# Sums of weights made by adding transfers one pair ahead, T2 ahead of T1, and three couples of the up product as two pairs of blocks

## The chip, the core and the metric

The kernel runs on one core of a Trainium2 chip. The engines named here are PE (TensorE, matrix products, with PEld its weight loads), DVE (VectorE), ACT (ScalarE), POOL (GpSimd) and SP (SyncE, which issues most transfers). The metric is the device time of one execution in microseconds (us); lower is better. Three executions of the kernel before took 824.05 to 824.6 us, with a median of 824.46.

## The reference

One layer of an encoder trunk on x of 512 tokens by 1024 features, all in float32. The weights of the large products are what the change touches.

```python
h = _rmsnorm(x, g_pre_mix)
proj = h @ w_in
q, k, v, g, u, sv, a_ret, a_sgu = jnp.split(proj, list(np.cumsum(IN_SPLITS)[:-1]), axis=-1)
y_ret = _retention_branch(q, k, v, g, ret_decay_logit, w_ret_o)
y_sgu = _sgu_branch(u, sv, sgu_ln_g, sgu_ln_b, w_spatial, b_spatial, w_sgu_o)
merged = jax.nn.sigmoid(a_ret) * y_ret + jax.nn.sigmoid(a_sgu) * y_sgu
x = x + _rmsnorm(merged @ w_out, g_post_mix)
h2 = _rmsnorm(x, g_pre_ffn)
x = x + _rmsnorm(_conv_gated_mlp(h2, w_up, conv_w, conv_b, w_down), g_post_ffn)
```

`_conv_gated_mlp` multiplies by `w_up` (1024 by 2 x 2816), runs a convolution of width 3 over the tokens, gates one half with the other and multiplies by `w_down` (2816 by 1024).

## The kernel before, in words

**Products.** Every float32 operand is split into a high and a low part (`split`, lines 84 to 86: ACT copies the high part, DVE subtracts it from the source), and a product is three matmuls: high x high, high x low, low x high.

**Pairs of blocks.** For u, the two gates, part of the up product and the down product, two blocks of outputs are computed together with seven products in place of eight (Winograd's form of Strassen's scheme). On the side of the weights that takes four blocks and four sums: T1 = B11 + B12, T2 = T1 + B22, T3 = B12 + B22, T4 = T2 + B21 (signs are put on the other side). `Pair` (line 676) runs the seven products of 12 matmuls of 256 columns each in three parts: `part1` four, `part2` one, `part3` two. A plain block is `f_block` (line 665): 24 matmuls of 512 columns.

**The stream of weights.** All weights lie in one array `wall` of 146 tiles of 128 x 1024. A list of `units`, written at lines 90 to 117, gives the order in which they are consumed: `("blk", i)` is a whole tile, a form such as `("T1", i)` is one block of a pair, `q` and `t` are the two units of a block of the down product. `w_get` (line 203) hands out the next unit and prepares those that follow, up to about nine slots of the tag `w4` (nine buffers: a form takes one, a `blk`, `q` or `t` two). Preparing means: SP loads into a tile of the tag `raw` (four buffers), the sums are added, and `split` writes the parts into slots.

- `w_form` (line 156): at `B11` SP loads both tiles of the pair, `a` and `b`. At `T1` DVE adds T1 (line 167) and T3 (line 168), and POOL adds T2 (line 169); at `T4` POOL adds T4 (line 171).
- `w_down` (line 177): `q` is a load of four quarters; `t` adds the fourth quarter to the first two in one DVE instruction (line 186) and two more sums of 256 columns (lines 190 and 191).

**Stages.** In order: q and k; v, sv and g with the retention; u as four pairs in a row, each with its `part3` put off until the next pair's `part1` is done; two gates with four rounds each (`gated_pair`: a pair and two plain blocks); the merge; the product with `w_out` (`Down`, line 818), six of whose eight weight tiles are kept ready; the up product; the down product in two halves of nine blocks, each with two whole tiles besides.

The first gate's results `r` are kept in eight SBUF tiles, and in the second gate POOL adds them (line 806).

**The up product.** It has 22 tiles; tiles 4 to 19 come in eight couples (`COUPLES`). In a couple the first tile is a pair of blocks and the second two plain blocks. `tile_done` then runs the convolution and the gate on DVE and ACT, and after tiles 7, 11, 13 and 17 also `down_forms`, which prepares activations for the down product.

**Order.** Each engine runs its own instructions in order; a transfer is issued by an engine's queue when the semaphores before it allow. Instructions are put in order, and tiles are given free buffers, by the compiler's scheduler.

Of the kernel before, what the change touches and what calls it, by code (L numbers as in the profile page):

```python
# [10 lines left out]
F32 = mybir.dt.float32  # L11
# [18 lines left out]
NBLK = 76  # L30
# [8 lines left out]
COUPLES = [(i, i + 1) for i in range(4, 20, 2)]  # L39

# [7 lines left out]
def tile_block(ctx: ExitStack, tc, xT, x, wall, par, cs, wsp, bsp, gpost, gffn, out):  # L48
# [43 lines left out]
    FORMS = ("B11", "B21", "T1", "T2", "T3", "T4", "B22")  # L92
    units = []
    i = 0
    while i < NW:
# [60 lines left out]
    def w_form(form, i):  # L156

        if form == "B11":
            a, b = raw_tile(), raw_tile()
            nc.sync.dma_start(a, wall[i])  # L160
            nc.sync.dma_start(b, wall[i + 1])
            w_raw["B11"], w_raw["B12"] = a[:, :S], a[:, S:]
            w_raw["B22"], w_raw["B21"] = b[:, :S], b[:, S:]
        elif form == "T1":
            t = raw_tile()
            w_raw["T1"], w_raw["T2"], w_raw["T3"], w_raw["T4"] = t[:, :S], t[:, S:], w_raw["B12"], t[:, S:]
            nc.vector.tensor_add(w_raw["T1"], w_raw["B11"], w_raw["B12"])  # L167
            nc.vector.tensor_add(w_raw["T3"], w_raw["B12"], w_raw["B22"])
            nc.gpsimd.tensor_tensor(out=w_raw["T2"], in0=w_raw["T1"], in1=w_raw["B22"], op=ALU.add)  # L169
        elif form == "T4":  # L170
            nc.gpsimd.tensor_tensor(out=w_raw["T4"], in0=w_raw["T2"], in1=w_raw["B21"], op=ALU.add)
        w = slot("wf", 0, 1088)
        lo, hi = w[:, AT_64 : AT_64 + S], w[:, S + AT_192 : 2 * S + AT_192]
        split(hi, lo, w_raw[form])
        return hi, lo

    def w_down(form, i):
# [5 lines left out]
        else:  # L183
            b, raw = w_raw["q"], raw_tile()
            two = "p (n c) -> p n c"
            nc.vector.tensor_tensor(
                out=raw[:, :512].rearrange(two, n=2), in0=b[:, :512].rearrange(two, n=2),
                in1=b[:, None, 768:].to_broadcast([P, 2, 256]), op=ALU.add,
            )
            nc.vector.tensor_add(raw[:, 512:768], raw[:, :256], b[:, 256:512])  # L190
            nc.vector.tensor_add(raw[:, 768:], raw[:, 512:768], b[:, 512:768])
        w = 768 if form == "q" else 1024
# [483 lines left out]
    class Pair:  # L676
# [27 lines left out]
        def part1(self):  # L704
# [616 lines left out]
```

## Time and profile before

| what | us |
|---|---|
| median of three executions | 824.46 |
| the profiled execution, device time | 827.49 |
| its span in the profile | 825.7 |
| PE busy in it | 815.4 |
| DVE busy | 661.4 |
| ACT busy | 440.8 |
| POOL busy | 101.0 |

The profile shows one execution, so terms worked out from it are made against its own time and then carried to the median. In a row of instructions the figures after the bar are the busy time in all, the mean of one in ns, and the idle time of the engine before them with what ended it. A matmul's own duration (277 ns for 256 columns) overlaps the next one; the time from one to the next is read from chains of them. "Landing" is the time from the issue of a transfer to its completion.

### The profile page before, as it was taken

To read this page: it belongs to the slowest core of one execution; us is meant where nothing else is said; L and a number is where in the kernel's file an instruction comes from. 1 tells how busy PE (TensorE), PEld (TensorE's weight loads), DVE (VectorE), ACT (ScalarE), POOL (GpSimd) and SP (SyncE) were. 2 spreads that over 40 slices of the span, in tenths; PEclk is the share of its full clock that TensorE was granted. 3 is DMA by queue.
4 is the path that set the end of the run, shared out by engine and by line. 5 is a ranking of instruction groups with operands and counts; after the bars stand their busy time and mean duration, and the time that the engine had idled before them with its cause. 6 is when DMAs were issued, how large, how long until landed. Compare 5 with 4: busy or idle time off the path is not lost.

```text
span 825.7 us, 13263 instructions
## 1 busy us (share of the span) xinstructions
PE 815.4 (99%) x5152; PEld 735.0 (89%) x5152; DVE 661.4 (80%) x1101; ACT 440.8 (53%) x771; POOL 101.0 (12%) x102
## 2 busy tenths in 40 slices
PE   9999999999999999999999999999999999999996
PEld 7888888888899999999988898899999998999996
DVE  7489897878797777767765568979899899988967
ACT  6636445546665444444445685556566566544531
POOL 0010000102121111132211211210111200000001
PEclk9999999999999999999999999999999999999999
DMA  8733222212223232222349111322322341233244
GB/s 294 246 116 102 77 77 77 77 52 78 90 102 129 103 102 80 101 101 103 108 166 339 48 55 55 103 102 103 102 103 102 102 154 52 77 115 129 96 147 154
DMA packets 29215, 93.24 MB, mean 113 GB/s; under 512 B 3360, under 2 KB 4000, under 8 KB 29152
## 3 DMA queue, kind: packets, MB, share of 16 engines
q1 hardware_dynamic: 26928, 86.85, 30.2%
q0 software_dynamic: 1360, 4.46, 1.6%
q10 hardware_dynamic: 864, 1.09, 0.4%
q8 instruction: 40, 0.66, 0.3%
q14 instruction: 23, 0.19, 0.1%
HBM read 88.19 MB, written 4.19 MB: 112 GB/s over the span
## 4 chain that ended last, share of the span: by engine, by line
PE 91%; DVE 6%; ACT 1%; issue 1%; DMA 0%; POOL 0%; DVEq 0%; SPq 0%; POOLq 0%; ACTq 0%
PE ps L692 23%; PE ps L217 12%; PE ps L218 12%; PE ps L219 12%; PE ps L1058 8%; PE ps L481 5%; PE ps L480 5%; PE ps L482 5%; PE ps L836 2%; PE ps L837 2%; PE ps L838 2%; PE ps L1074 1%; PE ps L761 1%; DVE fl L86 1%; PE ps L279 1%
## 5 line engine op out<-in xcount | busy, mean ns | idle before, releaser
L86 DVE TENSOR_TENSOR wl<-raw,wh 128x1024 fp32r<-128x1024 f32 (+1 forms) x93 | 109.1, 1182 | 48.9 <-PE ps L692 24.2
L79 ACT ACTIVATE wf<-raw 128x512 fp32r<-128x512 f32 x140 | 85.3, 627 | 102.7 <-PE ps L218 34.0
L86 DVE TENSOR_TENSOR wf<-raw,wf 128x512 fp32r<-128x512 f32 x140 | 111.1, 808 | 23.3 <-ACT wf L79 22.4
L692 PE MATMUL ps<-sh,wf 128*128 128x256 f32 x640 | 119.5, 277 | 0.0
L79 ACT ACTIVATE wh<-raw 128x1024 fp32r<-128x1024 f32 (+2 forms) x95 | 93.3, 993 | 37.4 <-DMA raw<-wall 17.0
L692 PEld LDWEIGHTS ps<-sh,wf 128*128 128x128 f32 x640 | 101.1, 188 | 0.8 <-ACT u L79 0.2
L217 PE MATMUL ps<-h2h,wh 128*128 128x512 f32 (+1 forms) x256 | 92.4, 363 | 0.7 <-ACT h2h L906 0.7
L218 PE MATMUL ps<-h2l,wh 128*128 128x512 f32 (+1 forms) x256 | 92.4, 363 | 0.0
L219 PE MATMUL ps<-h2h,wl 128*128 128x512 f32 (+1 forms) x256 | 92.1, 361 | 0.0
L692 PE MATMUL ps<-sl,wf 128*128 128x256 f32 x320 | 88.8, 278 | 0.0
L480 PE MATMUL ps<-wh,xh 128*128 128x512 f32 x192 | 75.0, 391 | 0.0
L481 PE MATMUL ps<-wl,xh 128*128 128x512 f32 x192 | 74.9, 390 | 0.0
L482 PE MATMUL ps<-wh,xl 128*128 128x512 f32 x192 | 74.8, 390 | 0.0
L169 POOL TENSOR_TENSOR raw<-raw,raw 128x512 f32<-128x512 f32 x20 | 36.2, 1809 | 235.2 <-DVE raw L167 207.8
L1058 PE MATMUL ps<-dl,fh 128*128 128x256 f32 x216 | 60.8, 281 | 0.1
L1058 PE MATMUL ps<-dh,fl 128*128 128x256 f32 x216 | 60.7, 281 | 0.0
L1058 PE MATMUL ps<-dh,fh 128*128 128x256 f32 x216 | 60.7, 281 | 0.0
L692 PEld LDWEIGHTS ps<-sl,wf 128*128 128x128 f32 x320 | 60.0, 188 | 0.6
L219 PEld LDWEIGHTS ps<-h2h,wl 128*128 128x128 f32 x256 | 48.0, 188 | 7.7
L217 PEld LDWEIGHTS ps<-h2h,wh 128*128 128x128 f32 x256 | 47.9, 188 | 7.9 <-ACT h2h L906 1.0
L692 PE MATMUL ps<-xh,wf 128*128 128x256 f32 x288 | 54.2, 278 | 0.0
L218 PEld LDWEIGHTS ps<-h2l,wh 128*128 128x128 f32 x256 | 48.0, 188 | 6.6
(314 smaller groups left out, 2048.9 us busy)
## 6 DMA issues: line engine op xcount, KB each, us to landing
raw<-wall SPq DMA_DIRECT2D x145, 512.0 KB, 3.6
x<-x SPq DMA_DIRECT2D x24, 256.0 KB, 5.9
xT<-xT SPq DMA_DIRECT2D x8, 256.0 KB, 5.4
x<-x POOLq DMA_DIRECT2D x8, 256.0 KB, 2.4
xT<-xT POOLq DMA_DIRECT2D x4, 256.0 KB, 3.6
out<-zg SPq DMA_DIRECT2D x4, 256.0 KB, 2.0
out<-zs ACTq DMA_DIRECT2D x3, 256.0 KB, 3.5
cs<-cs SPq DMA_DIRECT2D x2, 256.0 KB, 4.1
```

Of the source, the lines that this page charges most:

```text
L79: nc.scalar.activation(out=o, in_=i, func=AF.Copy)
L86: nc.vector.tensor_sub(lo, src, as32(hi))
L169: nc.gpsimd.tensor_tensor(out=w_raw["T2"], in0=w_raw["T1"], in1=w_raw["B22"], op=ALU.add)
L217: nc.tensor.matmul(o, ah, bh, start=start, stop=False)
L218: nc.tensor.matmul(o, ah, bl, start=False, stop=False)
L219: nc.tensor.matmul(o, al, bh, start=False, stop=stop)
L480: nc.tensor.matmul(acc[t], xh[k][:, c], wh[:, f], start=k == 0, stop=False)
L481: nc.tensor.matmul(acc[t], xh[k][:, c], wl[:, f], start=False, stop=False)
L482: nc.tensor.matmul(acc[t], xl[k][:, c], wh[:, f], start=False, stop=k == KD - 1)
L692: nc.tensor.matmul(o, w_[:, c], a_, start=first and k == n == 0, stop=k == 3 and n == 2, skip_group_check=True,)
L836: nc.tensor.matmul(o, ah, bh, start=k == 0, stop=False)
L1058: nc.tensor.matmul(o, a_[:, c], w_[:, f], start=j == t == i == 0, stop=j == DP - 1 and i == 2 and n not in (M2, M3, M4), skip_group_check= ...
```

## The change

Six things are done together.

1. *Sums by transfers.* T1 and T3 of a pair are no longer added by DVE. SP loads B11 and B12 side by side into a tile of a new tag `sum` (two buffers), and POOL issues a transfer that adds B12 and B22 to it (`accum_op`). This is asked for one pair ahead, at `B21` of the pair before. `b` keeps B22 in its first half; T2 is put in its second half, T4 in T1's place. In the down product the first two sums of `t` come in the same way, one block ahead. The tag `raw` goes from four buffers to three.
2. *Order of the forms.* T2 is prepared and used ahead of T1; POOL's T4 follows T1's split.
3. *Three couples as two pairs.* For the couples that begin at tiles 4, 8 and 14 (`BOTH`) the second tile is a `Pair` too, and `part3` and `tile_done` are put off until the next pair's `part1`.
4. *`r` goes to DRAM* through POOL's queue and is added in the second gate by an adding transfer instead of POOL's addition.
5. *Room.* `NBLK` goes from 76 to 74, two of the four `c` tiles of the down product move to the tag `tmp`, and the broadcast of `gffn` is asked for later.
6. On the host, the blocks of a pair are laid out as B11, B21 and B12, B22.

```diff
-NBLK = 76
+NBLK = 74
+BOTH = (4, 8, 14)
-    FORMS = ("B11", "B21", "T1", "T2", "T3", "T4", "B22")
+    FORMS = ("B11", "B21", "T2", "T1", "T3", "T4", "B22")
...
             for a, b in COUPLES:
                 pair = [(f, UP0 + 2 * a) for f in FORMS]
+                if a in BOTH:
+                    units += pair + [(f, UP0 + 2 * b) for f in FORMS]
+                    continue
...
+    w_pairs = [i for f, i in units if f in ("B11", "q")]
...
-        return sb.tile([P, 1024], F32, tag="raw", bufs=4, name=nm("raw"))
+        return sb.tile([P, 1024], F32, tag="raw", bufs=3, name=nm("raw"))
+
+    def sums(i, first, more):
+        if i not in w_sums:
+            t = w_sums[i] = sb.tile([P, 1024], F32, tag="sum", bufs=2, name=nm("sum"))
+            n = first.shape[1] * first.shape[2]
+            t = t[:, :n].rearrange("p (b c) -> p b c", b=2)
+            nc.sync.dma_start(t, first)
+            nc.gpsimd.dma_start(t, more, accum_op=ALU.add)
+        return w_sums[i]
+
+    def sums_ahead(i):
+        n = w_pairs.index(i) + 1
+        if n < len(w_pairs):
+            (form_sums if w_pairs[n] < DOWN0 else down_sums)(w_pairs[n])
+
+    def form_sums(i):
+        b, w = wall[i : i + 2, :, :S], wall[i + 1].rearrange("p (b c) -> p b c", b=2)
+        return sums(i, b.rearrange("b p c -> p b c"), w)
+
+    def down_sums(i):
+        w = wall[i].rearrange("p (b c) -> p b c", b=4)
+        return sums(i, w[:, 0:2], w[:, 3:4].to_broadcast([P, 2, 256]))
...
         if form == "B11":
-            a, b = raw_tile(), raw_tile()
+            a, b, t = raw_tile(), raw_tile(), form_sums(i)
             nc.sync.dma_start(a, wall[i])
-            nc.sync.dma_start(b, wall[i + 1])
...
-            nc.vector.tensor_add(w_raw["T1"], w_raw["B11"], w_raw["B12"])
-            nc.vector.tensor_add(w_raw["T3"], w_raw["B12"], w_raw["B22"])
+            nc.sync.dma_start(b[:, :S], wall[i + 1, :, S:])
...
+        elif form == "B21":
+            sums_ahead(i)
             nc.gpsimd.tensor_tensor(out=w_raw["T2"], in0=w_raw["T1"], in1=w_raw["B22"], op=ALU.add)
...
         split(hi, lo, w_raw[form])
+        if form == "T1":
+            nc.gpsimd.tensor_tensor(out=w_raw["T4"], in0=w_raw["T2"], in1=w_raw["B21"], op=ALU.add)
...
-            b, raw = w_raw["q"], raw_tile()
-            two = "p (n c) -> p n c"
-            nc.vector.tensor_tensor(
-                out=raw[:, :512].rearrange(two, n=2), in0=b[:, :512].rearrange(two, n=2),
-                in1=b[:, None, 768:].to_broadcast([P, 2, 256]), op=ALU.add,
-            )
+            b, raw = w_raw["q"], down_sums(i)
             nc.vector.tensor_add(raw[:, 512:768], raw[:, :256], b[:, 256:512])
             nc.vector.tensor_add(raw[:, 768:], raw[:, 512:768], b[:, 512:768])
+            sums_ahead(i)
...
-            self.product(2, self.s("S1"), True)
             o = self.product(0, self.s("S2"), False)
             copy(c1[:, T0], o)
+            self.product(2, self.s("S1"), True)
...
-    r = []
+    r = [dp_.tile([P, S], F32, tag=f"r{j}", name=f"r{j}") for j in range(KD)]
...
-            r.append(b)
+            nc.gpsimd.dma_start(r[2 * j + i], b)
...
-            nc.gpsimd.tensor_tensor(out=t, in0=t, in1=r[2 * j + i], op=ALU.add)
+            nc.gpsimd.dma_start(t, r[2 * j + i], accum_op=ALU.add)
...
+    late = []
+
+    def up_pair():
+        p = Pair(None, lambda: tmp("c"), (h2h, h2l, h2forms))
+        p.part1()
+        for j, q in late:
+            q.part3()
+            tile_done(j, q.t)
+        late.clear()
+        return p
...
         if i in couples:
-            p = Pair(None, lambda: tmp("c"), (h2h, h2l, h2forms))
-            p.part1()
+            p = up_pair()
+            if i in BOTH:
+                p.part2()
+                late.append((i, p))
+                p = up_pair()
+                p.part2()
+                late.append((i + 1, p))
+                i += 2
+                continue
...
-    c11, c12, c21, c22 = c4 = [blk(n="c") for _ in range(4)]
+    c11, c12, c21, c22 = c4 = [f(n="c") for f in (blk, blk, tmp, tmp)]
...
-    gpf = bcast(gffn, "gpf")
+    gpf = []
...
         products(m, j, steps if j == DP - 1 else {})
+        if j == 0:
+            gpf.extend(bcast(gffn, "gpf"))
```

More of the change, by code (lines that the diff above doesn't have):

```diff
@@ L792, in gated_pair @@
         return zip(o, p.t)
-    r = []
+    r = [dp_.tile([P, S], F32, tag=f"r{j}", name=f"r{j}") for j in range(KD)]
     for j in range(KD // 2):
-        for o, t in gated_pair(ogh, ogl, late if j == 0 else None):
+        for i, (o, t) in enumerate(gated_pair(ogh, ogl, late if j == 0 else None)):
             b = blk(n="r")
             v.tensor_mul(b, o, t)
-            r.append(b)
+            nc.gpsimd.dma_start(r[2 * j + i], b)
         mix(2 * j)
```

17 lines of the change are left out of this document (7 added, 10 removed).

## The prediction

> **What bounds the kernel now.** I read the page first, then PE's own waits, then the chain of waits, then stretches of the stage that the change shortens.
>
> ```profile
> span 825.7 us, 13263 instructions
> PE 815.4 (99%) x5152; PEld 735.0 (89%) x5152; DVE 661.4 (80%) x1101; ACT 440.8 (53%) x771; POOL 101.0 (12%) x102
> PE 91%; DVE 6%; ACT 1%; issue 1%; DMA 0%; POOL 0%; DVEq 0%; SPq 0%; POOLq 0%; ACTq 0%
> PE ps L264 <- DVE raw L259: 1.0, 1, 1.0
> PE ps L217 <- ACT h2h L906: 0.7, 1, 0.7
> PE ps L279 <- ACT wh L79: 0.4, 1, 0.4
> PE ps L624 <- DVE o L615: 0.3, 1, 0.3
> PE ps L605 <- DVE o L615: 0.3, 1, 0.3
> ```
>
> PE is busy in 815.4 of 825.7 us, and all its waits before the tail sum to 2.7 us. So the kernel goes faster only if PE gets fewer columns, and slower only if something new makes PE wait. DVE at 80% is an average; by stage:
>
> ```profile
> 541.05:561.55 20.50, 20.50 (x135) 18.56 (x134) 15.63 (x25) 11.14 (x20) 2.93 (x2) 1.00 0.29 103
> 561.55:582.05 20.50, 20.50 (x135) 18.56 (x134) 19.85 (x32) 12.71 (x23) 2.94 (x2) 1.00 0.26 92
> ...
> sum 82.00, PE 82.00 PEld 74.25 DVE 72.05 ACT 48.48 POOL 11.75; mean PE 20.50 PEld 18.56 DVE 18.01 ACT 12.12 POOL 2.94
> ...
> 10.00:20.00 10.00, 10.00 (x46) 8.18 (x45) 9.83 (x25) 8.50 (x12) 0.00 (x0) 1.00 0.92 331
> ...
> 217.00:262.00 45.00, 44.98 (x381) 44.78 (x380) 41.32 (x63) 29.25 (x54) 11.05 (x8) 1.00 0.31 106
> ...
> 734.00:806.00 72.00, 71.90 (x610) 71.91 (x611) 55.13 (x88) 31.93 (x48) 0.54 (x1) 1.00 0.36 126
> ```
>
> The columns are stretch, length, busy time of PE, PEld, DVE, ACT, POOL, granted clock, DMA share, GB/s. The first two rows are one couple of the up product each, and the sum is that of four: exactly 20.50 us a couple, PE never idle, at the full clock. DVE is at 15.6 to 19.9 us of it, the larger figure where `down_forms` falls into the couple. So PE sets the pace, with DVE close behind.
>
> **The couples: the term that pays.** In a couple one tile is a pair of blocks (7 products of 12 matmuls, 256 columns) and the other is two plain blocks (2 x 24 matmuls, 512 columns). For the couples that begin at tiles 4, 8 and 14 the change makes the second tile a pair too.
>
> ```profile
> 541.05 5.45 PE ps L692 x48
> ...
> 551.97 1.37 PE ps L692 x12
> ...
> 556.08 2.73 PE ps L692 x24
> ```
>
> Four products take 5.45, one 1.37, two 2.73: a pair costs 5.45 + 1.37 + 2.73 = 9.55 us. The couple is 20.50 us, so its two plain blocks cost 10.95 (0.228 us a matmul against 0.114: half the columns, half the time). A second pair in their place saves 10.95 - 9.55 = 1.40 us, and three couples save **4.2 us**.
>
> What must hide for that is the second pair's work on DVE.
>
> ```profile
> L86 DVE TENSOR_TENSOR wf<-raw,wf 128x512 fp32r<-128x512 f32 x140 | 111.1, 808 | 23.3 <-ACT wf L79 22.4
> L86 DVE TENSOR_TENSOR wl<-raw,wh 128x1024 fp32r<-128x1024 f32 x81 | 101.6, 1256 | 47.2 <-PE ps L692 24.2 <-issue 9.3 <-PE ps L218 4.8
> L167 DVE TENSOR_TENSOR raw<-raw 128x512 f32<-128x512 f32 x20 | 13.8, 688 | 1.5 <-DMA raw<-wall 1.4
> L168 DVE TENSOR_TENSOR raw<-raw,raw 128x512 f32<-128x512 f32 x20 | 17.1, 853 | 1.0 <-DMA raw<-wall 0.7
> L709 DVE TENSOR_TENSOR c<-ps,c 128x256 f32<-128x256 f32 x8 | 3.3, 417 | 0.0
> ```
>
> Seven splits at 0.808 replace two at 1.256, and three evacuations of 256 columns at 0.417 come in (L709, and its like at L720 and L732): 5.66 - 2.51 + 1.25 = +4.4 us. Against that, every pair loses its two DVE additions for T1 and T3, 0.688 + 0.853 = -1.54. Over the four couples above (two of them to be doubled, six pairs afterwards, four pairs' additions gone) DVE goes from 72.05 busy us to 72.05 + 2 x 4.4 - 4 x 1.54 = 74.7, while PE goes from 82.0 to 79.2. That is 94%: hidden, with 4.5 us to spare in four couples. Without that cover the gain shrinks by what DVE lacks (third rival). T2 before T1 in `part1` puts S2's product one product behind the copy of `b[0]` instead of two; 1.37 us covers an ACT copy of 256 columns. Deferring `part3` is what the u stage already does, and its row above (217 to 262) shows PE at 44.98 of 45. Both cost nothing.
>
> **T1 and T3 by transfers: what is queued behind what.** A pair now asks SP for 512 KB of first halves, and POOL for an adding transfer of 512 KB that waits for them; `b` shrinks to 256 KB. So a pair moves 1.75 MB instead of 1 MB: two in 19.1 us are 192 GB/s (512 KB and its like counted in 1024s), where the stretch from 10 to 20 us carries 331. No adding transfer is in this trace; the nearest rows are
>
> ```profile
> raw<-wall SPq DMA_DIRECT2D x145, 512.0 KB, 3.6
> ...
> xT<-xT SPq DMA_DIRECT2D x8, 256.0 KB, 5.4
> ...
> xT<-xT POOLq DMA_DIRECT2D x4, 256.0 KB, 3.6
> L884 POOL DMA_DIRECT2D x<-x x8: 542/568/589, 451.0 to 482.5; - x8
> L169 POOL TENSOR_TENSOR raw<-raw,raw 128x512 f32<-128x512 f32 x20 | 36.2, 1809 | 235.2 <-DVE raw L167 207.8
> L171 POOL TENSOR_TENSOR raw<-raw,raw 128x512 f32<-128x512 f32 x20 | 26.7, 1333 | 75.2 <-DVE wf L86 71.4 <-ACT cv L955 3.9
> L806 POOL TENSOR_TENSOR sig<-sig,r 128x512 f32<-128x512 f32 x8 | 11.6, 1465 | 36.4 <-DVE sig L805 36.4
> ```
>
> On POOL, T2(i) stands behind the adding transfer of pair i+1, which waits for a first half on SP, which waits for the sum tile that pair i-1 leaves at its T4 split. That round is 3.6 (load) + 0.57 (issue) + 1.81 (T2) + 2 x 0.81 (T2's and T1's splits) + 1.33 (T4) + 2 x 0.81 (T4's copy on ACT, put at DVE's time, and its split) = 10.6 us, against 9.55 us of PE a pair where pairs follow pairs. Such a run is at most four pairs (the u stage), so it loses 3 x 1.05 = 3.2 us out of a lead of seven products (nine slots, two held by the deferred pair), 7 x 1.365 = 9.6 us, of which the unit's own copy and split take some 2. Cost 0; 3.2 us with that lead gone.
>
> The `r` tiles go to DRAM and come back as an adding transfer: 3.6 or more for POOL's 1.465 (L806). Only the last two matter, for mh[6] and mh[7]. `Down` first runs 48 matmuls over k = 0 and 1, 48 x 0.228 = 10.9 us, so this is hidden; uncovered, with a landing of 3.6 to 7.2, it would cost 2 to 6 us once.
>
> **The start.** Three `raw` tiles instead of four, one of them `hold`.
>
> ```profile
> 3.05 0.43 SPq L133 DMA_DIRECT2D raw<-wall  x1
> ...
> 7.86 0.33 SPq L133 DMA_DIRECT2D raw<-wall  x1
> 8.23 0.43 SPq L241 DMA_DIRECT2D xT<-xT  x1
> ...
> 5.23 1.17 PE L279 MATMUL ps<-xh,wh 128*128 128x512 f32 x4 [0.44 <-ACT wh L79]
> ```
>
> The load at 3.05 now waits until 7.86, when block 0's tile is free, and xT[2] behind it on SP. With 3.6 to 4 us to land and a copy and a split of at most 1.26 each it is ready near 14.4. PE needs it after two blocks of 24 x 0.228, at 5.23 + 10.9 = 16.2. Cost 0; bounds -0.3 (the blocks ahead land sooner) and +0.5 (a landing as slow as xT's 5.4, with xT's own split behind the block's).
>
> **The down product: the tight place.** The first two sums of each `t` unit come by transfer (L186, 0.69 us of DVE, 18 times, off PE's path: PE is busy throughout). In return the ring of two sum tiles closes on itself: the `t` split of block j-1 frees the tile; SP loads 256 KB; POOL's transfer adds 256 KB; then DVE's two additions, ACT's and DVE's split of block j+1.
>
> ```profile
> L1141 SPq DMA_DIRECT2D x<-x x8: 320/372/452, 795.6 to 816.4; - x8
> ...
> DMA to landing us min/median/max: 2.8/4.5/5.4
> ...
> 741.47 0.43 DVE L190 TENSOR_TENSOR raw<-raw,raw 128x256 f32<-128x256 f32 x1
> ...
> 743.57 1.23 DVE L86 TENSOR_TENSOR dl<-raw,dh 128x1024 fp32r<-128x1024 f32 x1 [1.21 <-ACT dh L79]
> ...
> 752.71 0.85 ACT L79 ACTIVATE dh<-raw 128x768 fp32r<-128x768 f32 x1 [1.76 <-PE ps L1058]
> ...
> 757.65 0.85 ACT L79 ACTIVATE dh<-raw 128x768 fp32r<-128x768 f32 x1 [1.76 <-PE ps L1058]
> ```
>
> A lone 256 KB load lands in 2.8. The add lands in 3.6 (POOL's plain load, issue included) plus an unknown d. From the first addition to the end of the split are 744.80 - 741.47 = 3.3. Together 9.7 + d us per two blocks; PE takes 2 x (757.65 - 752.71) = 9.88. So the ring fits as long as d is under 0.2 and otherwise falls behind by d - 0.2 every two blocks, 4.5 times in each half of nine blocks. The lead it can eat is three units of 2.47 less a copy and a split of 1.23 each, 5.0 us (nine slots are four units in flight, and a unit's second half waits for the oldest of them); in the first half the two whole blocks add 2 x 48 x 0.114 = 10.9. Bounds for d: 0 (no dearer than a plain load) and 3.6 (a second transfer in full). I take **0.8**, what a second 256 KB costs within one load (3.6 for 512 KB against 2.8), because an add reads as much again: behind by 4.5 x 0.6 = 2.7 us, within the lead, cost 0. At d = 3.6 it is 4.5 x 3.4 - 5.0 = +10.3.
>
> The Trainium skill bears on d. In "Collectives: The Full Stack", section "The bandwidth ceiling: the fold count and why AG ≠ RS ≠ AR", the reduce in a transfer is limited not by the addition but by having two sources to read. By that rule an add costs what a load of twice its size costs, and the sum stays at 820.2, where the upper bound, two transfers in full, would give 830.5; no run here shows it yet.
>
> **The sum.** The profiled execution took 827.49 us: its span of 825.7 and 1.8 around it. It is 3.0 above the median of 824.46. Couples -4.2, all else 0: 821.5 of span, 823.3 for such an execution, and by the median 824.46 - 4.2 = **820.2 us**. Removing the additions could also shorten the two 0.3 us waits on L615; the range's low end takes them, not the sum.
>
> **The rivals.** *The ring of sum tiles in the down product sets the pace (slower).* For it: 9.7 against 9.88 leaves no room, and DVE, being in order, holds other splits behind an addition that waits. Against it: it needs d above 2.3 to eat the gain (4.5 x 2.1 - 5.0 = 4.4) and above 2.6 to end slower by 0.2%. At d = 3.1, 4.5 x 2.9 - 5.0 = 8.0 us: 820.2 + 8.0 = **828**. *POOL's order gives part back in the runs of pairs.* For it: T2 stands behind a wait for two engines. Against it: a lead of 7.6 us. If first halves land at xT's 5.4 and an issue for two rows a partition takes 1.14, the round is 13.0, a pair loses 3.4, three rounds 10.3: 2.7 us are given back, **823**, and up to 824 if the `r` transfers add to it. *DVE binds the doubled couples, and the change doesn't do what it says.* A split beside a POOL addition takes up to 1.78 us instead of 0.69:
>
> ```profile
> L86 DVE TENSOR_TENSOR wf<-raw,wf x140: 674/686/1782, 191.9 to 668.1; 128x512 fp32r<-128x512 f32 x140
> ```
>
> The mean of 0.808 charges that about once a pair; four times a doubled couple at the full 1.1 us adds 3 x 1.1 = 3.3 us to each, so the 4.5 us to spare in four couples with two doubled ones are overdrawn by 2.1, half of the gain or more: **822.3 to 824.5**. The Trainium skill ("SBUF — State Buffer", section "Who interferes with whom") has a DVE instruction with two SBUF inputs fully blocked by a GpSimd one that reads SBUF; the row's 1782 agrees, and T2 and T4 stay on POOL in the new pairs.
>
> **How the numbers follow.** As worked out 60% (818.8 to 822.3); POOL's order 11%; DVE 7%; the ring 18%; something at the start or in the smaller pool of blocks 4%, slower. A change under 0.2%, 1.6 us, can't be told from none. Faster (below 822.8): the first case and a few per cent of the next two, 0.64. Same: most of the second and third, 0.13. Slower: the ring and the last case, 0.23. The range, 818.8 to 828.2, holds the first three cases and the ring up to d = 3.1.
>
> **What would show it.** Doubled couples of 19.1 us with PE never idle, 1.4 shorter each. DVE below 95% there. The adding transfers of 256 KB landing within 4.9 us in the down product (3.6 and a d of up to 1.3), and no PE wait on a DVE split of `dl` there; PE still 99% busy. Wrong would be: PE waits of over 1 us on `wf` or `dl` splits, DVE waits for a DMA into `sum` that repeat from block to block, or the first 20 us growing longer.

## The result, and the profile after

The changed kernel takes 864.58 us (median of four executions, 863.55 to 871.38) against 824.25 us: over all executions a ratio of 1.0508, with a 95% interval of 1.0453 to 1.0562. It is 5% slower, where the prediction had 820.2 us and a range that ended at 828.2.

Lines of the page of the changed kernel, the last four of them transfers with their size and the median us to landing:

```profile
span 861.9 us, 13751 instructions
PE 825.2 (96%) x5260; PEld 746.6 (87%) x5260; DVE 637.1 (74%) x1067; ACT 446.6 (52%) x798; POOL 153.5 (18%) x157
...
sum<-wall SPq DMA_DIRECT2D x23, 512.0 KB, 4.2
sum<-wall POOLq DMA_DIRECT2D x23, 512.0 KB, 5.7
...
sum<-wall SPq DMA_DIRECT2D x18, 256.0 KB, 3.4
sum<-wall POOLq DMA_DIRECT2D x18, 256.0 KB, 4.8
```

And the largest of its waits on PE and one on DVE (in all, times, longest, in us):

```profile
PE ps L716 <- ACT c L80: 11.3, 6, 4.1
PE ps L1100 <- DVE dl L87: 8.2, 5, 3.2
PE ps L716 <- ACT sig L80: 3.4, 1, 3.4
PE ps L1100 <- ACT dh L80: 2.6, 2, 2.1
...
DVE sum L213 <- DMA sum<-wall: 26.0, 9, 6.2
```

PE waited 2.7 us before the tail in the kernel before; here four groups alone make 25.5 us, and they name three places. `c L80` is ACT's copy out of PSUM in the up product, `sig L80` the same copy in the second gate, `dl` and `dh` the splits of the down product. DVE has become less busy (637.1 against 661.4 us): no engine has become the bound; the engines wait for each other.

The time by stages, for the two kernels and the experiments below. A stage runs from the start of its first matmul to that of the next stage's, read from the PE records of each profile; in brackets is the idle time between matmuls (pauses over 0.15 us).

| kernel | u | second gate | couples | down product | span |
|---|---|---|---|---|---|
| before | 45.7 | 76.6 | 161.8 (0) | 112.2 (0) | 825.7 |
| after | 44.2 | 81.9 (3.4) | 175.8 (11.3) | 128.9 (11.5) | 861.9 |
| E1 T1 first | 44.1 | 76.6 | 166.6 (4.9) | 127.9 (11.5) | 848.6 |
| E2 four raw tiles | 52.7 (5.2) | 76.8 | 180.8 (17.3) | 132.6 (13.2) | 876.2 |
| E3 down sums on DVE | 45.0 | 81.4 (3.0) | 175.7 (10.9) | 113.7 (1.3) | 845.7 |
| E4 no doubled couples | 45.5 | 81.2 (2.7) | 161.8 (0) | 131.0 (11.9) | 852.1 |
| E5 T1 first, down sums on DVE | 45.9 | 76.6 | 166.9 (4.5) | 110.5 (1.0) | 829.7 |
| E6 before, doubled couples | 44.6 | 76.6 | 180.2 (12.7) | 109.3 (0.4) | 840.8 |
| E7 before, T2 first | 45.9 | 76.6 | 167.3 (4.5) | 109.0 (0) | 829.5 |
| E8 E1 with three sum tiles | 43.9 | 76.8 | 168.1 (6.8) | 123.6 (8.8) | 843.1 |
| E9 E5, doubled at 4, 10, 16 | 44.7 (0.4) | 78.8 (1.8) | 161.8 (0.8) | 109.1 (0) | 824.4 |
| E10 E5, T2 first in three pairs | 43.9 | 76.6 | 166.7 (5.2) | 110.3 (1.1) | 827.0 |
| E11 E9, T2 first in three pairs | 45.7 | 76.6 | 163.6 (2.7) | 109.1 (0) | 824.7 |
| E12 E8, asked for two blocks ahead | 44.1 | 76.6 | 168.0 (6.7) | 124.9 (10.1) | 846.4 |
| E13 before, T2 first in one u pair | 43.8 | 76.6 | 161.6 (0) | 109.0 (0) | 821.1 |
| E14 E9, T2 first in one u pair | 43.5 | 76.6 | 162.4 (1.6) | 109.1 (0) | 821.4 |
| E15 E1 without the down add | 45.7 | 76.6 | 167.3 (5.9) | 111.8 (0) | 831.3 |

From before to after the span grows by 36.2 us: couples +14.0, down product +16.7, second gate +5.3, u -1.5, all other stages together +1.7. In each of the three stages that grow, the idle time is less than the loss. Most of the rest is the clock: behind these pauses the granted clock falls to half for a while. Two stretches of the same length, behind the pause of 3.53 us at 588 us and a little later (columns as in the prediction's tables of stretches):

```profile
591.70:596.50 4.80, 4.80 (x23) 4.80 (x24) 4.31 (x7) 2.66 (x5) 0.00 (x0) 0.50 0.67 228
597.00:601.80 4.80, 4.80 (x35) 4.43 (x34) 3.87 (x5) 2.95 (x5) 1.20 (x2) 1.00 0.73 241
```

PE counts as busy in both. The first holds 23 matmuls of 256 columns, one every 0.21 us where the full clock gives one every 0.114; the second holds 25 of 256 columns and 10 of 512. The records of the granted clock have six such windows before the tail, five of 3.4 us and one of 6.8. They hold 102 matmuls of 256 columns, each 0.1 us longer than at the full clock: some 10 us that no term of the prediction held. In the second gate and the down product pauses and clock make up nearly all of the loss (3.4 + 1.6 of 5.3 us, 11.5 + 4.5 of 16.7). In the couples they are 11.3 + 4.1 us, against 4.1 us of columns saved; the 2.7 us that are left are a slower pace of PE (last section) and the shortest waits.

**Where PE waits in the couples.** The timeline of the changed kernel around 588 us, first PE, then ACT, then DVE (start, length, instruction, and in brackets the idle time before it with its releaser):

```profile
591.53 0.58 PE L716 MATMUL ps<-sh,wf 128*128 128x256 f32 x1 [3.53 <-ACT c L80]
...
586.92 1.68 ACT L979 ACTIVATE cv<-c,part 128x512 f32<-128x512 f32 x2
588.51 0.36 ACT L80 ACTIVATE c<-ps 128x256 f32<-128x256 f32 x1
588.77 1.04 ACT L80 ACTIVATE wh<-raw 128x1024 fp32r<-128x1024 f32 x1
590.57 0.63 ACT L993 ACTIVATE cv<-cv 128x512 f32<-128x512 f32 x1 [0.76 <-DVE cv L986]
591.11 0.37 ACT L80 ACTIVATE c<-ps 128x256 f32<-128x256 f32 x1
...
587.77 1.93 DVE L982 SCALAR_TENSOR_TENSOR cv<-c,part,cv 128x511 f32<-128x511 f32 x1
589.73 0.75 DVE L986 SCALAR_TENSOR_TENSOR cv<-c,part,cv 128x511 f32<-128x511 f32 x1
```

The product with B21 ended near 588. S2's product comes next and goes into `b[0]`, so it needs the copy of B11's product, which could have run from 586.6 on. But that copy (at 591.11) stands at its place in ACT's order: behind two convolution steps (L979), the copy of an earlier product, a split, and a GELU (L993). The GELU waits for a convolution step on DVE (L986), itself late because L982 took 1.93 us instead of the 0.74 it takes at 590.40; POOL's addition of T4 (L202) ran beside it from 587.56 to 589.13. So what the prediction's third rival speaks of, DVE slowed beside POOL, is one link of this chain, though DVE's work as a whole does not set the pace. The copy takes 0.37 us and is some 4 us late.

### The profile page after: what moved, and what is told of

Its sections match the earlier page's. It is cut to its first block, busy times and chain, and to the rows that moved or that the text cites. A ratio compares the mean times of both kernels' runs of the same rounds, so it can differ in the third digit from the quotient of the medians.

```text
span 861.9 us, 13751 instructions
## 1 busy us (share of the span) xinstructions
PE 825.2 (96%) x5260; PEld 746.6 (87%) x5260; DVE 637.1 (74%) x1067; ACT 446.6 (52%) x798; POOL 153.5 (18%) x157
## 5 line engine op out<-in xcount | busy, mean ns | idle before, releaser
L716 PE MATMUL ps<-sh,wf 128*128 128x256 f32 x736 | 142.1, 284 | 11.3 <-ACT c L80 11.3
L716 PEld LDWEIGHTS ps<-sh,wf 128*128 128x128 f32 x736 | 119.8, 194 | 13.7 <-ACT c L80 12.4
L80 ACT ACTIVATE wh<-raw 128x1024 fp32r<-128x1024 f32 (+2 forms) x89 | 87.0, 987 | 32.9 <-DMA raw<-wall 19.9
L137 POOL DMA_DIRECT2D sum<-wall x41 | 42.4, 1034 | 273.9 <-DMA sum<-wall 152.6
L87 DVE TENSOR_TENSOR wf<-raw,wf 128x512 fp32r<-128x512 f32 x92 | 66.2, 733 | 25.5 <-ACT wf L80 25.3
L80 ACT ACTIVATE wf<-raw 128x512 fp32r<-128x512 f32 x92 | 56.2, 624 | 47.7 <-PE ps L242 23.8
L241 PE MATMUL ps<-h2h,wh 128*128 128x512 f32 (+1 forms) x208 | 73.5, 357 | 0.7 <-ACT h2h L930 0.7
L242 PE MATMUL ps<-h2l,wh 128*128 128x512 f32 (+1 forms) x208 | 73.7, 356 | 0.1
L80 ACT ACTIVATE wf<-sum 128x512 fp32r<-128x512 f32 x69 | 43.0, 627 | 57.8 <-PE ps L716 34.5
L87 DVE TENSOR_TENSOR wf<-sum,wf 128x512 fp32r<-128x512 f32 x69 | 52.7, 770 | 14.2 <-ACT wf L80 13.9
L197 POOL TENSOR_TENSOR raw<-sum,raw 128x512 f32<-128x512 f32 x23 | 41.9, 1822 | 58.0 <-DMA raw<-wall 31.5
```

Of the source, the lines that this page charges most:

```text
L80: nc.scalar.activation(out=o, in_=i, func=AF.Copy)
L87: nc.vector.tensor_sub(lo, src, as32(hi))
L137: nc.gpsimd.dma_start(t, more, accum_op=ALU.add)
L241: nc.tensor.matmul(o, ah, bh, start=start, stop=False)
L242: nc.tensor.matmul(o, ah, bl, start=False, stop=False)
L716: nc.tensor.matmul(o, w_[:, c], a_, start=first and k == n == 0, stop=k == 3 and n == 2, skip_group_check=True,)
```

## The experiments

Every experiment is the changed kernel or the kernel before with the edits shown; ratios are to the kernel before, timed on the same chip.

### E1, E3, E4, E2: one part at a time

E1 puts T1 ahead of T2 again.

```diff
-    FORMS = ("B11", "B21", "T2", "T1", "T3", "T4", "B22")
+    FORMS = ("B11", "B21", "T1", "T2", "T3", "T4", "B22")
...
+            self.product(2, self.s("S1"), True)
             o = self.product(0, self.s("S2"), False)
             copy(c1[:, T0], o)
-            self.product(2, self.s("S1"), True)
```

> The changed kernel with T1 ahead of T2 again, in the list of forms and in the products of part1; all else as changed. Theory Q (order): PE loses time in the couples because the product of S2 now comes one product (1.37 us) after the one whose copy by ACT it needs, and that copy stands in ACT's queue behind a gelu or a split that waits; then PE's waits on ACT's copies of c (11.3 us in the changed kernel) fall below 3, the couples fall from 175.8 to about 160 us and the whole to about 848. Theory R (ring of raw tiles): the weights themselves come late, because three raw tiles make the load of b wait for POOL's T4; then the waits move to the splits and the time stays within 4 us of 864.

Measured 850.59 us, 1.0306 (1.0276 to 1.0336). The second gate is back at 76.6 and the couples fall by 9.2 us, PE's waits for ACT's copy from 11.3 to 3.7 us. The order cost 14.5 us in these two stages. The couples still stand 4.8 us above before and 6.6 above the 160 that theory Q expected, so the order is not the whole cause there.

E3 adds the first two sums of the down product on DVE again, into the same two tiles.

```diff
-    w_pairs = [i for f, i in units if f in ("B11", "q")]
+    w_pairs = [i for f, i in units if f == "B11"]
...
-            b, raw = w_raw["q"], down_sums(i)
+            b, raw = w_raw["q"], sb.tile([P, 1024], F32, tag="sum", bufs=2, name=nm("sum"))
+            two = "p (n c) -> p n c"
+            nc.vector.tensor_tensor(
+                out=raw[:, :512].rearrange(two, n=2), in0=b[:, :512].rearrange(two, n=2),
+                in1=b[:, None, 768:].to_broadcast([P, 2, 256]), op=ALU.add,
+            )
...
-            sums_ahead(i)
```

> The changed kernel, but in the down product the first two sums are added by DVE again, into the same two sum tiles, with no transfer. Theory S (the ring of sum tiles there closes too slowly): the stage from the first down product to the last falls from 128.8 to about 112 us, the whole to about 847. Rival (more traffic or the three raw tiles hold the loads back): it stays above 122.

Measured 845.52 us, 1.0244 (1.0184 to 1.0305). The down product falls from 128.9 to 113.7 us, and the other stages stay within 1 us of the changed kernel.

E4 has `BOTH = ()`.

> The changed kernel with no couple doubled (BOTH empty). If the loss in the couples comes with the doubled ones (deferred tile_done, more splits, theory D), the couples take 162 to 165 us instead of 175.8 and the whole about 853. If it comes from the sums by transfer or the order wherever they are, it stays above 170.

Measured 856.68 us, 1.0379 (1.0296 to 1.0463). Without doubled couples the stage is 161.8 us, exactly that of before, although T2 still stands ahead of T1. So in the changed kernel the order hurts the couples where pair follows pair.

E2 gives `raw` its four buffers back; for room `NBLK` is 72.

> The changed kernel with four raw tiles instead of three (and NBLK 72 to make room). Theory R: the couples fall by 10 us or more, and the 3.4 us gap at the last gate round (ACT waits there for a transfer into raw) goes with its slow clock: about 847. Theory Q: the couples stay at 173 to 176, only the gap at the gate goes, 5 us: about 859.

Measured 876.98 us, 1.0625 (1.0589 to 1.0661): slower than either theory gave, so the three raw tiles are not the cause of the couples' loss. The second gate is back at 76.8 us, though T2 still stands first: there the fourth raw tile does help. With it the losses move to ACT's queue in other places, u among them (52.7 us), and one of them shows the mechanism at its plainest. PE's largest waits in E2, and ACT at 544 us:

```profile
PE ps L716 <- ACT c L80: 17.3, 6, 5.9
...
PE ps L716 <- ACT u L80: 5.2, 1, 5.2
```

```profile
544.38 0.63 ACT L80 ACTIVATE wf<-sum 128x512 fp32r<-128x512 f32 x1 [7.63 <-POOL sum L202]
544.91 0.36 ACT L80 ACTIVATE c<-ps 128x256 f32<-128x256 f32 x1
```

ACT stood idle for 7.63 us, since the instruction at the head of its queue, the split of T4, waited for POOL's addition; the copy that PE needed was next in line. POOL in turn had stood 5.17 us waiting for an adding transfer into `sum`, ahead of T2 and T4; the pause of 5.2 us in u (`u L80`) has the same chain, with 4.83 us of waiting on POOL. Of this E2 shows the chain, not why it is worse here than with three raw tiles.

### E5 to E7: do the parts add up, and what does each do to the kernel before?

E5 is E1 and E3 together.

> The changed kernel with T1 back ahead of T2 and the first two sums of the down product back on DVE; transfers for the other pairs' sums and for r, and the three doubled couples, stay. If the two losses (order Q, ring of sum tiles S) are separate, the stages are those of the two runs before: second gate 76.6, couples 166.6, down product 113.7, in all 848.6 - (127.9 - 113.7) = 834 us of span, 836 us of time. If the ring's lateness in the down product came out of the couples (a rival), taking the order back would have cured part of it twice and the sum of the stages is higher, 840 or more. Neither theory makes it faster than the kernel before (824.3).

Measured 831.18 us, 1.0067 (1.0036 to 1.0099). E1 saved 14.0 us and E3 19.1, and 864.58 - 33.1 is 831.5: as far as the spread of these runs shows, the two losses are separate and add up. The span is 829.7 for the expected 834: the first tiles of the up product (ahead of the couples), 2.9 us longer in E1 than before, are back at their length, the down product is 3.2 us shorter than in E3 (PE's pace, last section), and u 1.8 longer.

E6 is the kernel before with the doubled couples alone: `BOTH`, `up_pair` and `late` as in the change, T1 ahead of T2, all sums by DVE and POOL.

> The kernel before with the three doubled couples alone (T1 ahead of T2, all sums by DVE and POOL, part3 put off as in the change). The term of the prediction, PE alone: couples 161.8 - 4.2 = 157.6, time 820. Theory D (DVE): with T1 and T3 still on DVE, each doubled couple adds 4.4 us for the second pair and 1.54 for its additions, so four couples with two doubled ask 72.05 + 2 x 5.94 = 83.9 us of DVE against 79.2 of PE: DVE then sets the pace there, couples 163 to 165, time 826 to 828.

Measured 843.05 us, 1.0214 (1.0185 to 1.0244), a bigger loss than either theory gave. PE's waits in E6:

```profile
PE ps L696 <- ACT c L80: 10.5, 10, 2.0
PE ps L696 <- DVE wf L87: 2.2, 4, 0.6
```

The couples take 180.2 us. With the sums by transfers (E5) they take 166.9. E5 differs by the transfers and what came with them (three raw tiles, `r` by DRAM, less room). So the transfers do help the up product, by 13 us in this setting; they make room for an edit that does not pay. And the waits are again mostly for the copy, with T1 first: the order is not the only way to expose it.

E7 is the kernel before with T2 ahead of T1 alone.

> The kernel before with T2 ahead of T1 alone (list of forms and part1), no transfers of sums, no doubled couples. Prediction's term: 0, time 824.3. Theory Q (the copy of b[0] is only one product ahead and stands in ACT's queue): exposed where something stands ahead of it on ACT, so the second gate gets its gap of 3 us and its stretch at half clock, +5, while the couples, whose pairs do not follow pairs, stay at 161.8: 829. If instead the gap of the second gate needs the transfers or three raw tiles too, it stays at 824 to 825.

Measured 832.87 us, 1.0097 (1.0064 to 1.0130). The second gate stays at 76.6, so its loss in the changed kernel needs something else of the change as well; E2, where it is gone, points to the three raw tiles. The couples grow by 5.5 us, of which four waits for ACT's copy make 4.5 (2.3 the longest). So on the kernel before, with T1 and T3 on DVE, the order hurts even where a plain block follows each pair; with the sums by transfers it does not (E4).

### E9 to E11: why the doubled couples still lose with T1 first

The change puts doubled couples at tiles 4, 8 and 14; `down_forms` runs after tiles 7, 11, 13 and 17, and falls into the couples at 8 and 14. In E5 PE and ACT at 574 us:

```profile
574.29 0.39 PE L720 MATMUL ps<-sh,wf 128*128 128x256 f32 x1 [1.30 <-ACT c L80]
...
570.98 0.63 ACT L80 ACTIVATE wf<-sum 128x512 fp32r<-128x512 f32 x1 [3.24 <-POOL sum L202]
571.52 0.62 ACT L80 ACTIVATE fh<-gp 128x512 fp32r<-128x512 f32 x1
572.04 0.36 ACT L80 ACTIVATE c<-ps 128x256 f32<-128x256 f32 x1
572.30 0.62 ACT L80 ACTIVATE wf<-raw 128x512 fp32r<-128x512 f32 x1
572.83 0.62 ACT L80 ACTIVATE fh<-fs 128x512 fp32r<-128x512 f32 x1
573.34 0.62 ACT L80 ACTIVATE wf<-raw 128x512 fp32r<-128x512 f32 x1
573.86 0.37 ACT L80 ACTIVATE c<-ps 128x256 f32<-128x256 f32 x1
```

PE waits for the copy at 573.86; ahead of it stand a split that waited 3.24 us for POOL, and `down_forms`' splits (`fh`) among those of the weights. By the order of PE's records the product that waits is S2's of the second pair: S3 of the first pair starts at 567.49, B11 and B21 of the second fill 569.02 to 571.40 (four matmuls of B11 stand ahead of S3), S1 starts at 571.40 and S2 at 574.29. It needs the copy of its own pair's B11, done by 570.1, with two products between. S3 of the first pair, right behind S2 and into the same `b[0]`, waits 0.3 us only. Theory G below takes the waiting product for S3's, which the records do not bear out.

E9 is E5 with `BOTH = (4, 10, 16)` (the first part of the diff below), E10 is E5 with T2 ahead of T1 in the first pair of each doubled couple alone (the other parts), E11 is both.

```diff
-BOTH = (4, 8, 14)
+BOTH = (4, 10, 16)
...
-                    units += pair + [(f, UP0 + 2 * b) for f in FORMS]
+                    units += [(f, UP0 + 2 * a) for f in FORMS2] + [(f, UP0 + 2 * b) for f in FORMS]
...
-            p = up_pair()
+            p = up_pair(i in BOTH)
             if i in BOTH:
```

> The kernel of the run with T1 first and the down product's sums on DVE, with the doubled couples at tiles 4, 10 and 16 in place of 4, 8 and 14. There the couples at 8 and 14 are the ones into which down_forms falls (after tiles 7 and 13); the new places have none. Theory F (the burst of down_forms on DVE and ACT makes the copies late): the waits of 4.5 us in the couples mostly go and the couples fall from 166.9 to 160 or less, time 825. Theory G (a doubled pair has S3 right behind S2, both into b[0], with the copy of b[0] between them, wherever it stands): the couples stay at 165 or more, time 830.

> The kernel of the run with T1 first and the down product's sums on DVE; only the first pair of each doubled couple takes T2 ahead of T1, so that the product with S1 stands between S2 and S3. Doubled couples stay at 4, 8 and 14. Theory G: the two waits of 1.3 and 1.4 us before the S3 products go, couples 166.9 - 2.7 = 164, time 828. Theory F, and the reading of the order in the changed kernel (a copy one product ahead is late wherever ACT has a queue): the waits only move from S3 to S2, couples 166 to 168.

> Both edits of the two runs before together. PE's columns alone give 157.6 for the couples (161.8 - 4.2). If F and G each hold a part of the 9.3 us over that, the couples come to 158 to 161 and the time to 821 to 824.5, at or just under the kernel before (825.3 on the chip of the last runs). If the pace of PE or DVE is what is left, 163 or more.

E9 measured 826.02 us, 1.0024 (1.0003 to 1.0046), its couples 161.8; E10 830.63, 1.0090 (1.0067 to 1.0112), couples 166.7; E11 826.35, 1.0025 (1.0007 to 1.0042), couples 163.6. The place is worth 5 us, as theory F has it, although the 160 us or less that F expected were not reached. The order inside the first pair is worth nothing. E10's edit leaves the product that waits in E5, S2 of the second pair, as it was: it still waits 0.6 and 1.0 us, and S2 of the first pair now waits as well (0.35 and 0.93). So theory G was not tested at the place that costs. Both together (E11) are no better than the place alone, and the 158 to 161 us hoped for did not come.

In E9 the stage has the 4.1 us of columns less and is as long as before all the same. Going from the start of one matmul to the next, intervals that are over 0.15 us too long make 1.7 us of the difference, and 3.0 us are spread over all the others: a slower pace of PE in its runs of pairs, of which the last section tells.

### E8, E12, E15: the down product

One round of a sum tile in the changed kernel, SP, POOL, DVE and ACT, from the load of its first half to the next load:

```profile
799.17 0.33 SPq L136 DMA_DIRECT2D sum<-wall  x1
803.37 1.22 POOL L137 DMA_DIRECT2D sum<-wall  x1 [3.69 <-DMA sum<-wall]
808.36 0.42 DVE L213 TENSOR_TENSOR sum<-sum,raw 128x256 f32<-128x256 f32 x1
809.41 1.06 ACT L80 ACTIVATE dh<-sum 128x1024 fp32r<-128x1024 f32 x1 [2.36 <-DVE sum L214]
810.50 1.23 DVE L87 TENSOR_TENSOR dl<-sum,dh 128x1024 fp32r<-128x1024 f32 x1 [1.26 <-ACT dh L80]
811.75 0.33 SPq L136 DMA_DIRECT2D sum<-wall  x1
```

First half 4.2, add 5.0, additions and splits 3.4: 12.6 us for a tile that serves every second block, and PE needs two blocks in 9.9. This is one of the shorter rounds: from load to load of the same tile they take 11.3 to 19.3 us in this stage, waits for their turn included.

E8 is E1 with three sum tiles (`NBLK` 72), E12 the same with the sums of the down product asked for two blocks ahead.

```diff
-            t = w_sums[i] = sb.tile([P, 1024], F32, tag="sum", bufs=2, name=nm("sum"))
+            t = w_sums[i] = sb.tile([P, 1024], F32, tag="sum", bufs=3, name=nm("sum"))
...
-        n = w_pairs.index(i) + 1
-        if n < len(w_pairs):
-            (form_sums if w_pairs[n] < DOWN0 else down_sums)(w_pairs[n])
+        n = w_pairs.index(i)
+        for j in w_pairs[n + 1 : n + 2 + (i >= DOWN0)]:
+            (form_sums if j < DOWN0 else down_sums)(j)
```

> The changed kernel with T1 ahead of T2 and three sum tiles instead of two (for that NBLK is 72). Theory S, the round of a sum tile: one round was measured as 12.6 us (first half 4.2 with POOL's wake-up, add 5.0, additions and splits 3.4); for two blocks PE takes 9.9, for three 14.8. With three tiles the ring no longer limits: down product 112 to 114 us instead of 127.9. If the loss lies in the order of waits on DVE, ACT or POOL and not in the number of tiles, it stays above 122. The stages before it may be longer by the smaller pool of blocks; only the down product is read here.

> The kernel with T1 first and three sum tiles, with the sums of the down product asked for two blocks ahead instead of one. With three tiles alone the down product fell only from 127.9 to 123.6, because a request stood behind the block before it in the order of SP. If the lead of the request is what lacks (first half 4.2, add 5.0, additions and splits 3.4 = 12.6 us against 9.9 us for two blocks and 14.8 for three), the down product comes to 112 to 114. If the transfers themselves are too slow, or POOL's and SP's queues hold them up in any order, it stays above 120.

E8 measured 846.36 us, 1.0255 (1.0210 to 1.0300), its down product 123.6 us where 112 to 114 were expected; E12 851.09, 1.0315 (1.0221 to 1.0410), down product 124.9. So neither a third tile nor an earlier request cures it, against the round's own sum. What DVE does in E12:

```profile
790.35 0.43 DVE L213 TENSOR_TENSOR sum<-sum,raw 128x256 f32<-128x256 f32 x1 [4.91 <-DMA sum<-wall]
790.69 0.95 DVE L87 TENSOR_TENSOR dl<-raw,dh 128x768 fp32r<-128x768 f32 x1
791.56 0.42 DVE L214 TENSOR_TENSOR sum<-sum,raw 128x256 f32<-128x256 f32 x1
...
793.64 1.22 DVE L87 TENSOR_TENSOR dl<-sum,dh 128x1024 fp32r<-128x1024 f32 x1
```

The addition of the next block (L213, at 790.35) stands ahead of the splits of the block that PE wants. It waits 4.91 us for its transfer, and the splits, which free the tiles of SP's next loads, stand behind it. DVE waits at L213 in the same way in the changed kernel (26.0 us in all) and in E8 (28.4). That the compiler's scheduler put it so early in E12 because the tile is free earlier is likely, but not shown.

E15 is E1 with the adding transfer left out in the down product.

```diff
-            nc.gpsimd.dma_start(t, more, accum_op=ALU.add)
+            if i < DOWN0:
+                nc.gpsimd.dma_start(t, more, accum_op=ALU.add)
```

> The changed kernel with T1 first; in the down product the adding transfer is left out, so that its first two sums lack the fourth quarter. The first halves still come by SP into two sum tiles. One round of a sum tile with the add measured 12.6 us against 9.9 of PE for two blocks; without it 4.2 (or the landing of 3.5 alone) + 3.4 = 7 to 8 us, so by theory S the down product falls from 127.9 to 109 to 113. If SP's order (a first half behind a load of raw that waits for its tile) is what holds, it stays above 120.

Measured 833.05 us in one execution, down product 111.8 us with no pause. SP's part and its order stayed, and DVE's waits at its additions fell to 2.0 us at most. So the adding transfer, with its issue on POOL, is what makes this stage long; how much of that goes by the length of the round and how much by DVE's queue is open, since three tiles should have cured the first.

### E13, E14: the pace of PE, and the best of both

E13 is the kernel before with T2 ahead of T1 in the first pair of u alone; E14 is E9 with the same edit.

```diff
-            units += pair
+            units += [(f, i) for f in FORMS2] if i == U0 else pair
...
-            p.part1()
+            p.part1(j == 0)
```

> The kernel before with T2 ahead of T1 in the first pair of the u stage alone. Theory P (pace): in a run of 256-column products without plain blocks, one short wait of PE (in the kernel before 0.30 us at 222.4, for ACT's copy of b[0], S3 right behind S2) leaves PE at 118 ns a matmul instead of 113.6 until a plain block or a longer pause comes. With S1 between S2 and S3 the wait does not arise: the stage of 336 matmuls goes from 45.7 to about 44.2 us, as it did in the changed kernel, and the time by -1.5 to 822 to 823.5, the first version under the kernel before. If the pace in the u stage depends on something else (DVE's sums beside it, the transfers), u stays at 45.7 and the time unchanged.

> The changed kernel with T1 first, the down product's sums on DVE, the doubled couples at 4, 10 and 16 (826.0 against 823.8), and T2 ahead of T1 in the first pair of u alone. By theory P u falls from 44.7 to 43.8 to 44.2; with the second gate at 76.6 (it had a wait of 1.8 us) the span is 821.5 to 823.5 and the time within 1.5 us of the kernel before. If the order of ACT's queue changes elsewhere, 825 to 828 as before.

E13 measured 823.51 us, 0.9997 (0.9984 to 1.0009); E14 824.84, 1.0005 (0.9987 to 1.0023). In E13's profile u takes 43.8 us, as theory P has it, but the time does not differ from the kernel before beyond its interval. No version was found that beats it; E14, with the columns saved and all that was found put right, equals it; its couples take 162.4 us, so the saving is not seen there either.

## Why the prediction was wrong, step by step

Three terms that the prediction put at nothing failed: the cover of the doubled couples, the order T2 before T1, and the ring of sum tiles. The stages of the first two grew by 14.0 us (couples) and 5.3 (second gate), that of the third by 16.7 (down product).

- **The columns of the doubled couples, -4.2: right as a count.** In the profiles the couples have 672 matmuls of 256 columns and 372 of 512 before, 924 and 228 after (the last 12 of the stage's last plain block are not in it). At the pace the prediction used (0.114 and 0.228 us) that is 161.4 against 157.3: 4.1 us less.
- **"Hidden, with 4.5 us to spare in four couples": the first failed step.** It weighed DVE's sum of work against PE's. What ran out was not work but order: ACT's copies of 0.37 us stood behind instructions that waited for DVE or POOL. E4 against the changed kernel prices the edit there at +14.0 us; against the couples before, it is +4.8 with T1 first (E1), and 0 away from `down_forms` (E9). Two terms were missing for the gain to come: the burst of `down_forms`, 5 us, and PE's pace, 3.0 us in E9. The u row quoted in the prediction, 381 matmuls in 45.00 us, is 118 ns each; the couple's products, 48 in 5.45, are 113.5. A second pair makes the couple a run of pairs like u, and the sum priced it by the other row.
- **"T2 before T1 ... Both cost nothing": the second failed step.** "1.37 us covers an ACT copy of 256 columns" is true of the copy and not of its place in the queue. Going back gains 9.2 us in the couples and 5.3 in the second gate (E1); alone, the order costs 5.5 us of the couples (E7). In the second gate the copy stood behind three splits of `w_out` that waited for a load:

```profile
416.73 0.63 ACT L80 ACTIVATE mh<-sig 128x512 fp32r<-128x512 f32 x1 [4.33 <-DMA sig<-r]
...
423.22 2.09 ACT L80 ACTIVATE wh<-raw 128x512 fp32r<-128x512 f32 x3 [3.61 <-DMA raw<-wall]
425.22 0.36 ACT L80 ACTIVATE sig<-ps 128x256 f32<-128x256 f32 x1
```

- **The ring of sum tiles, "within the lead, cost 0": the third failed step, and the rival with the right place, given 18%.** The term that was mis-sized is the round, 9.7 + 0.8 = 10.5 us in the prediction and 12.6 in the trace. The first half was put at 2.8, a lone load; with the other loads it takes 3.4 in the median and 4.2 until POOL's add goes out. The add's landing of 4.4 (4.8 measured, d = 1.2) was not far off. With 12.6 the prediction's own formula gives 4.5 x (12.6 - 9.9) - 5.0 = 7 us; PE's pauses were 11.5, and half clock added some 4.5. So the formula has the place right but not the whole: either the lead was overrated or most rounds were longer than this one, and by it three tiles (14.8 us for three blocks) would have cost nothing, where E8 still lost 11.4 us. By the rule that the prediction carried over from the Trainium skill ("Collectives: The Full Stack", section "The bandwidth ceiling: the fold count and why AG ≠ RS ≠ AR", where it stands for the reduce of a ring between cores) an add is as dear as a load of twice its size, 4.2 us for a 512 KB load here; the 256 KB add took 4.8, so the rule was nearer than two loads in full (6.8).
- **POOL's order in the run of u's pairs, `r` by DRAM, the start: cost 0, right in most runs.** In E5 and E11, with all three still in, u, the second gate and the first 217 us are within 0.4 us of before. Two runs say where the margin ends. In E2 u took 52.7 us, for a wait on POOL's order as its rival has it. In E9 the second gate had one pause of 1.8 us, again behind three splits that waited for a load. A share of `r` in the second gate's loss is not excluded either: ACT waited 4.33 us for its transfer just ahead of those splits (416.73 above), though in E2 a wait of 4.54 us at this place cost nothing.
- **A pause priced by its length: missing throughout.** Some 10 us of the 36 come from half clock behind pauses. The Trainium skill has the rule ("TensorE: Matmul & The Clock Gate", section "Why this matters for your kernels": no idle gaps over about 3 us between bursts of matmuls, or the clock drops to half). The trace agrees for the pauses of 3.4, 3.5, 4.1 and 3.2 us; windows also followed groups of shorter ones (1.36 and 1.87 us within 11 us in the down product) and a lone 2.03 us in E4, while a lone 2.3 in E7 and 2.5 in E8 had none.

The prediction named the signs under which it would be wrong, and two of them came: PE waits of over 1 us on `dl`, and DVE waits for transfers into `sum` that repeat from block to block.

## What to carry to other kernels

A copy out of PSUM is only as early as the slowest instruction ahead of it on its engine: when products are reordered, count what stands in that queue and what it waits for, not the copy's own length, and keep at least two products of room where the queue holds splits of weights (E5 lost 1.3 us at a product that had two). A ring of tiles fed by two transfers in a row is to be priced with landings under load and with the issuing engine's wake-up, and every addition that waits for it holds up the splits behind it. Each pause of PE of some 3 us cost half as much again in clock here (1.6 us a window of 3.4), so a change that saves half a percent of the columns' time cannot afford one.

## What the runs showed of the hardware

PE has two paces for back-to-back matmuls of 256 columns, at a granted clock of 1.00 and without a pause. The u stage of E10 and of E15, with the same order of products, and the down product of the kernel before and of E7, where the code is the same:

```profile
224.00:260.00 36.00, 36.00 (x320) 36.00 (x319) 29.58 (x48) 24.05 (x45) 11.76 (x9) 1.00 0.73 198
```

```profile
224.00:260.00 36.00, 36.00 (x305) 36.00 (x305) 27.84 (x46) 23.42 (x43) 11.19 (x9) 1.00 0.70 191
```

```profile
755.00:815.00 60.00, 60.00 (x512) 60.00 (x512) 47.30 (x83) 24.95 (x46) 1.66 (x3) 1.00 0.33 115
```

```profile
755.00:815.00 60.00, 60.00 (x531) 60.00 (x531) 49.06 (x82) 26.84 (x46) 1.10 (x2) 1.00 0.35 118
```

That is 112.5 against 118.0 ns a matmul, and 117.2 against 113.0. In the records a run mostly keeps its pace for tens of microseconds, and the changes found stand at a pause or where the kind of product changes: in the kernel before at 222.4 us, behind a pause of 0.30 us ahead of S3's first product, the pace turned from fast to slow. It did so in E11 and E15 as well, left the pace alone in E6, E8 and E10, and in E1, E9 and E12, which began u at 119 ns a matmul, turned it from slow to fast: such a pause can set the pace either way and need not. E13 took it away, and u ran at 113.6 (331 matmuls in 37.60 us). What decides was not found. It is worth 3 us in the down product (112.2 against 109.0). The executions of the kernel before fall into two groups, 13 from 822.66 to 824.43 and 10 from 825.29 to 827.81 us beside E13, and the execution profiled for the prediction, 827.49, has the slow pace there; that the pace makes the groups is likely but not shown, as no execution of the faster group was profiled.

An adding transfer took 4.8 us for 256 KB and 5.7 for 512 KB in the median, against 3.4 and 4.2 for the plain loads into the same tiles, and its issue kept POOL 0.86 to 1.25 us.
